# Row scaling of a softmax: from VectorE to GpSimd for all but the last three groups

## The chip, the cores and the metric

The kernel runs on one core of one Trainium2 chip. The time is device time in microseconds (us). Every ratio compares runs with a granted clock of 1.0. The *span* is the length of the profiled execution; the measured time is some 1.9 us longer. A *period* is the time from the start of one group of rows to the start of the next on the same engine.

## The reference

```python
x = randn(16, 1024, 512)                      # float32
x_max = np.max(x, axis=-1, keepdims=True)
exp_x = np.exp(x - x_max)
out = exp_x / np.sum(exp_x, axis=-1, keepdims=True)
```

It is 16384 independent softmax rows of 512 values: 33.55 MB in, 33.55 MB out.

## The kernel before

The kernel handles 128 softmax rows at a time, one per partition. Such a slab of 128 x 512 values is called a "row" from here on, and there are 128 of them. They come in ten chunks of 3, 5, 8 and then 16 rows, all into one big tile `held` that is worked on in place. Chunks are cut into groups of at most 8 rows, which makes 17 groups, numbered 0 to 16. Per group VectorE takes the negated maxima, ScalarE the exponentials with their sums, VectorE the reciprocals and then, row by row, the scaling. Loads are issued from SyncE. Stores are issued from ScalarE's own stream, so ScalarE's exponentials stand behind a store that waits.

```python
CHUNKS = [(3, 0), (5, 3), (8, 8), (16, 16), (16, 32), ...]   # rows, place in held
GROUP = 8
FINISH_BEFORE = (1, 2, 3)          # finish the small chunks before the next one starts
STORE_ROWS = {3: 8, 4: 8, 5: 8}    # these chunks are stored in halves, the later ones whole

    def rowmax(g):   # VectorE
        nc.vector.reduce_max(out=shift[g], in_=place[k][:, a:b, :], axis=AX, negate=True)

    def exps(g):     # ScalarE, one instruction per row
        for r in range(a, b):
            nc.scalar.activation(..., func=EXP, bias=shift[g][...], accum_out=sums[g][...])

    def scale(g):
        nc.vector.reciprocal(out=recip, in_=sums[g])
        for r in range(a, b):
            nc.vector.tensor_scalar_mul(out=place[k][:, r, :], in0=place[k][:, r, :],
                                        scalar1=recip[:, r - a : r - a + 1])
        if since is not None:
            nc.scalar.dma_start(out=dst[k][:, since:b, :], in_=place[k][:, since:b, :])
        # ... (the last two loads are issued behind two of the stores)

        for g in ...:              # the main loop
            # ... (for the small chunks, scale(waiting) comes first)
            rowmax(g); exps(g)
            if waiting is not None: scale(waiting)     # the group before
            waiting = g
        scale(waiting)
```

## Time and profile before

| | before |
|---|---|
| time, median of 6 fast runs | 161.48 us |
| span | 159.6 us |
| busy: VectorE (DVE), ScalarE (ACT), GpSimd (POOL) | 123.9, 93.3, 0.2 us |
| DMA | 67.13 MB, 421 GB/s on average over the span |
| last store issued | 144.93 us |

Engine names in the profile are DVE for VectorE, ACT for ScalarE, POOL for GpSimd. The prediction below shows the lines of this profile and how they are read.

### The profile page before, as it was taken

How to read it: one execution, taken by the hardware profiler on the slowest of the kernel's cores; microseconds unless marked ns; L12 is line 12 of the kernel's file. 1: busy time of each engine (PE TensorE's matmuls, PEld its weight loads, DVE VectorE, ACT ScalarE, POOL GpSimd, SP SyncE). 2: the span in 40 equal slices, each digit the busy share in tenths (PEclk: the TensorE clock that was granted, in tenths of full speed). 3: DMA queues.
4: the chain of work that ended last, by engine and by line, in shares of the span. 5: the costliest groups of instructions: out<-in, count | busy, mean ns of one | idle time of the engine just before them, and what ended most of it. 6: DMA issues, size and time to landing. Idle time of an engine off the chain costs nothing.

```text
span 159.6 us, 511 instructions
## 1 busy us (share of the span) xinstructions
DVE 123.9 (78%) x162; ACT 93.3 (58%) x257; POOL 0.2 (0%) x4
## 2 busy tenths in 40 slices
DVE  0482880799699999999999999999999999853000
ACT  0717119207994959595958687776868595940000
POOL 0000000000000000000000000000000000000000
DMA  7999999899999999999899999999999999999993
GB/s 267 443 456 432 399 414 466 375 404 467 411 446 411 485 419 396 439 411 493 378 448 439 411 497 411 405 444 402 435 444 485 411 402 468 435 402 419 485 411 164
DMA packets 3315, 67.13 MB, mean 421 GB/s; under 512 B 368, under 2 KB 368, under 8 KB 624
## 3 DMA queue, kind: packets, MB, share of 16 engines
q1 hardware_dynamic: 1440, 33.56, 49.4%
q10 hardware_dynamic: 1872, 33.56, 49.0%
q14 instruction: 3, 0.02, 0.0%
HBM read 33.55 MB, written 33.55 MB: 421 GB/s over the span
## 4 chain that ended last, share of the span: by engine, by line
DVE 71%; ACT 14%; issue 3%; DMA 3%; DVEq 0%; ACTq 0%
DVE shift L125 39%; DVE held L147 30%; ACT held L133 14%; DMA held<-in_x_dram 3%; DVE recip L145 2%; DVEq L199 0%; ACTq L133 0%
## 5 line engine op out<-in xcount | busy, mean ns | idle before, releaser
L133 ACT ACTIVATE held<-held,shift 128x512 f32<-128x512 f32 x128 | 90.5, 708 | 43.4 <-DVE shift L125 33.3
L125 DVE TENSOR_REDUCE shift<-held 128x8 f32<-128x4096 f32 (+2 forms) x17 | 70.7, 4164 | 4.6 <-DMA held<-in_x_dram 4.6
L147 DVE TENSOR_SCALAR held<-held,recip 128x512 f32<-128x512 f32 x128 | 52.2, 482 | 0.6
L133 ACT ACTIVATION_READ_ACCUMULATOR held<-held,shift 128x1 f32 x128 | 23.9, 187 | 0.0
L145 DVE RECIPROCAL recip<-sums 128x8 f32<-128x8 f32 (+2 forms) x17 | 3.3, 195 | 15.8 <-ACT held L133 15.8
L133 ACT ACT_TABLE_LOAD x1 | 1.3, 1283 | 4.7 <-DMA held<-in_x_dram 4.7
L188 POOL MEMSET const-bfloat16-1.0<- 128x1 bf16 x1 | 0.1, 103 | 0.0
L188 POOL MEMSET const-uint8-127<- 128x1 uint8 x1 | 0.1, 102 | 0.0
L188 POOL MEMSET const-float32-1.0<- 128x1 f32 x1 | 0.1, 100 | 0.0
L188 POOL MEMSET const-float32-0.0<- 128x1 f32 x1 | 0.1, 99 | 0.2 <-issue 0.2
## 6 DMA issues: line engine op xcount, KB each, us to landing
held<-in_x_dram SPq DMA_DIRECT2D x7, 4096.0 KB, 41.8
out_dram<-held ACTq DMA_DIRECT2D x4, 4096.0 KB, 20.9
out_dram<-held ACTq DMA_DIRECT2D x7, 2048.0 KB, 35.3
held<-in_x_dram SPq DMA_DIRECT2D x1, 2048.0 KB, 11.7
held<-in_x_dram SPq DMA_DIRECT2D x1, 1280.0 KB, 7.2
out_dram<-held ACTq DMA_DIRECT2D x1, 1280.0 KB, 19.9
held<-in_x_dram SPq DMA_DIRECT2D x1, 768.0 KB, 4.6
out_dram<-held ACTq DMA_DIRECT2D x1, 768.0 KB, 15.6
```

The costliest lines, as they stand in the source:

```text
L125: nc.vector.reduce_max(out=shift[g], in_=place[k][:, a:b, :], axis=AX, negate=True)
L133: nc.scalar.activation(out=place[k][:, r, :], in_=place[k][:, r, :], func=EXP, bias=shift[g][:, r - a : r - a + 1], scale=1.0, accum_out=s ...
L145: nc.vector.reciprocal(out=recip, in_=sums[g])
L147: nc.vector.tensor_scalar_mul(out=place[k][:, r, :], in0=place[k][:, r, :], scalar1=recip[:, r - a : r - a + 1],)
L188: nc = _bacc.Bacc("TRN2", target_bir_lowering=False, num_devices=1)
```

## The change

The intent is to relieve VectorE, which heads the chain of work, by an engine that does nothing: GpSimd multiplies a whole group by its reciprocals in one instruction, with the reciprocal of each row repeated along the row by a step of 0 in the access pattern. The last three groups stay on VectorE.

```diff
+ON_VECTOR = 3
 ...
         nc.vector.reciprocal(out=recip, in_=sums[g])
-        for r in range(a, b):
+        on_pool = g < len(groups) - ON_VECTOR
+        if on_pool:
+            nc.gpsimd.tensor_tensor(
+                out=place[k][:, a:b, :],
+                in0=place[k][:, a:b, :],
+                in1=recip.unsqueeze(2).to_broadcast([P, b - a, d]),
+                op=mybir.AluOpType.mult,
+            )
+        for r in () if on_pool else range(a, b):
             nc.vector.tensor_scalar_mul(
```

## The prediction

> **What bounds the kernel now.** I read the page first (engine shares, slices, queues), then the chain that ended last, the timeline of the last 20 us, and a table of stretches. From the page:
>
> ```profile
> span 159.6 us, 511 instructions
> DVE 123.9 (78%) x162; ACT 93.3 (58%) x257; POOL 0.2 (0%) x4
> DMA  7999999899999999999899999999999999999993
> q1 hardware_dynamic: 1440, 33.56, 49.4%
> q10 hardware_dynamic: 1872, 33.56, 49.0%
> L133 ACT ACTIVATE held<-held,shift 128x512 f32<-128x512 f32 x128 | 90.5, 708 | 43.4 <-DVE shift L125 33.3
> L125 DVE TENSOR_REDUCE shift<-held 128x8 f32<-128x4096 f32 (+2 forms) x17 | 70.7, 4164 | 4.6 <-DMA held<-in_x_dram 4.6
> L147 DVE TENSOR_SCALAR held<-held,recip 128x512 f32<-128x512 f32 x128 | 52.2, 482 | 0.6
> ```
>
> GpSimd is free and VectorE is the busiest engine, so moving 128 multiplications off it looks like an easy gain. But the load queue (q1) and the store queue (q10) together hold the 16 DMA engines for 49.4 + 49.0 = 98.4% of the span. The kernel must move 2 x 33.56 MB whatever computes it. VectorE's chain and the transfers are balanced: both are nearly full.
>
> The chain of work, in order of time, repeats one period for as long as there are rows:
>
> ```profile
> 23.20 0.02 issue
> 23.23 5.75 ACT held L133 x16
> ...
> 69.33 4.33 DVE shift L125
> 73.66 0.12 DVE recip L145
> 73.78 0.02 issue
> 73.81 3.26 DVE held L147 x8
> 77.07 4.33 DVE shift L125
> ```
>
> A group of 8 rows costs VectorE 4.33 (maximum) + 0.14 (reciprocal) + 3.26 (scaling) = 7.73 us; ScalarE needs 5.75 us for its exponentials. So VectorE sets the pace of the stores: 2.10 MB in 7.73 us is 271 GB/s, less than the DMA engines move, but loads use the rest. The stretches show it:
>
> ```profile
> 60.00:100.00 40.00, 39.82 (x55) 30.09 (x85) 0.00 (x0) 1.00 1.00 432
> 100.00:130.00 30.00, 29.86 (x39) 22.07 (x62) 0.00 (x0) 1.00 1.01 435
> 130.00:145.00 15.00, 12.36 (x23) 9.37 (x28) 0.00 (x0) 1.00 0.98 424
> 145.00:160.00 15.00, 0.00 (x0) 0.00 (x0) 0.00 (x0) 1.00 0.83 356
> ```
>
> (Columns after the stretch: its length; busy VectorE, ScalarE, GpSimd; clock; DMA share; GB/s.) In the last stretch 356 GB/s x 15 us = 5.34 MB still moves. The last store, of 4.19 MB, is issued at 144.93 by the timeline:
>
> ```profile
> 141.64 3.26 DVE L147 TENSOR_SCALAR held<-held,recip 128x512 f32<-128x512 f32 x8
> 144.93 0.34 ACTq L153 DMA_DIRECT2D out_dram<-held  x1
> ```
>
> So only 5.34 - 4.19 = 1.15 MB, or 2.7 us at 430 GB/s, is queued ahead of it. That is the whole slack: **a last store that is issued over 2 to 3 us later moves the end one for one.** With an empty queue I estimate the end at issue + 13.5 us: 9.8 us of transfer (4.19 MB at 430 GB/s), about 2.2 us from the last packet to the end of the span (the queue is quiet from about 157.4 to 159.6), and about 1.5 us to start.
>
> **What the Trainium skill says.** (1) "GPSIMD Engine Reference", section 3.1: tensor_tensor at N = 2048 fp32 takes 4497 ns on GpSimd, against 2293 on VectorE, about 2.6 cycles per element at 1.2 GHz, because both inputs share one read port. A broadcast second input is still a second input. The trace before has no GpSimd arithmetic (4 memsets), so it can't confirm this. (2) "SBUF — State Buffer", "Who interferes with whom": GpSimd's port pair is VectorE's second pair, an exclusive lock for a whole instruction; tensor_scalar in a 2-port mode takes it, tensor_reduce never does on trn2. The trace agrees that the scaling is in a two-element mode: 3.26 us for 8 x 512 elements is 0.80 ns each, the maximum 4.33 us for 4096, 1.06 ns each. (3) The same page, "A bandwidth-pool intuition that's wrong": 436 GB/s is the ceiling of DMA to SBUF; it also gives about 358 GB/s for HBM. The trace has 432 to 435, so it sits at the first and above the second.
>
> **The change, part by part.**
>
> *Removed from VectorE*: 14 of 17 scalings, 104 of 128 rows; 104 x 0.407 us (3.26/8) = 42.3 us. The maxima (70.7), reciprocals (3.3) and 24 rows of scaling (9.8) stay: 84 us. VectorE stops being the pace: 4.5 us per full group.
>
> *Added on GpSimd*: two groups of 1536 and 2560 elements and twelve of 4096. My estimate from (1): 4096 x 2.6 / 1.2 GHz = 8.87 us, plus 0.06 (4497 less 4437, the fixed part of the same row), plus a hop between engines: **D = 9.0 us per 8 rows**. That replaces 3.26 us of VectorE. GpSimd then needs 13 x 9.0 = 117 us for its 104 rows, more than any engine before in one period: 9.0 against 7.73.
>
> *Moved*: the instruction order shows that stores stay in ScalarE's stream and now wait for GpSimd; the exponentials behind them wait too. That matters at the start, where each small chunk is finished before the next one's exponentials.
>
> Walking through it: reciprocal of group 0 at 8.84 (as before); GpSimd 3 rows, 3.4, to 12.3; exponentials of the next 5 rows 3.64, to 16.0; reciprocal 16.2; GpSimd 5.6, to 21.9; exponentials 5.75, to 27.7; GpSimd from 27.9 to 36.9; exponentials to 42.7; fourth group on GpSimd 42.9 to 51.9. From there exponentials (5.75) hide under GpSimd (9.0), and ten more groups follow without a gap: the last GpSimd group ends at 51.9 + 90 = 141.9, the one before at 132.9.
>
> The tail: ScalarE's store of the eighth chunk waits until 132.9, then come the exponentials of group 14 (from 0) to 138.7 and its reciprocal at 138.9. Its VectorE scaling meets the last GpSimd group, which holds the lock until 141.9: it runs 141.9 to 145.2. The maximum of group 16 stands behind it: 149.5. Exponentials to 155.3, reciprocal and scaling to 158.8: **last store at 158.8**, 13.9 us later than before. If there is no lock, 3 us less: 155.8. The ninth chunk's store goes out at about 145.3 and is through by 157.1, so the last one finds an empty queue. End of the span: 158.8 + 13.5 = 172.3, or 169.3 without the lock. The measured time is 161.46 - 159.6 = 1.9 above the span: 174.2 or 171.2. I say **173.0 us**, 7.1% slower.
>
> **The rivals.**
>
> *A: GpSimd is quick enough and nothing happens.* If the multiplication ran near one element per cycle (D about 4.5), or anything up to about 7.7, GpSimd would keep VectorE's old pace, and the transfers would still set the end: 160 to 162 us. For it: the added instruction is one per 8 rows, so dispatch is paid once, and one input is a broadcast. Keeping just three groups on VectorE suggests that the author didn't think GpSimd starved. Against: the page lays the cost on two inputs, not on dispatch.
>
> *B: VectorE was the real limit and DMA merely keeps it company, so it gets faster.* The chain speaks for it (71% VectorE). Against: DMA is at 424 to 435 GB/s in every stretch from 10 to 145 us. At 436 throughout, 67.1 MB need 153.9 us, plus some 2 us at each end, plus 1.9: about 160 us, 1% at best. Over 2% (158.2) is nearly excluded.
>
> *C: GpSimd is dearer than the page's row*, by the lock, the in-place write, or the broadcast pattern. Each 0.1 us on D is carried by 12 full-group equivalents between the start and the last store but one (3 + 5 + 11 x 8 = 96 rows): 1.2 us at the end. D = 10 makes 185 us. A one-time cost before GpSimd's first multiplication (there is one extra setup instruction ahead of it) would add up to its own length, unless it runs in the idle 8.8 us at the start, as I expect.
>
> **Range and chances.** The end is 173.0 + 12 x (D - 9.0), until the floor of about 161. D between 8.4 and 9.7 gives 166 to 181; with 1.5 us each way for the lock I take 164 to 182. Slower by over 2% means over 164.7, D above about 8.3: I give 0.83. A floor result (rival A) has 0.15, faster 0.02.
>
> **What would show the steps right or wrong.** Right: GpSimd over 110 us busy, its 4096-element instructions starting 9.0 us apart from about 43 us on; stores following them; VectorE near 84 us busy; idle DMA slices from about 130 us on; the last store issued at 156 to 159; the first tensor_scalar of group 14 held until GpSimd's last instruction ends. The maxima should keep their 4.33 us beside GpSimd, since they take no second port. Wrong: a GpSimd spacing below 7.7 us with the DMA slices full to the end (A); a span under 157 us with DMA above 436 GB/s (B); a spacing of 10 or more, or a long first multiplication (C). If the spacing is 9.0 but the last store isn't late, my order of waits is wrong, most likely in which exponentials stand behind a store.

## The result

The changed kernel takes 161.47 us (median of 6), the kernel before 161.48. The ratio is 0.9998, with a 95% interval of 0.9985 to 1.0011. (A ratio here is the mean time of one kernel's fast runs over that of the other's of the same rounds, so not quite the ratio of the medians.) It is the same time to a tenth of a per cent; the prediction of 173 us was wrong.

The time is equal, but the inside is not. The page of the changed kernel:

```profile
span 159.6 us, 442 instructions
DVE 82.6 (52%) x58; ACT 92.9 (58%) x257; POOL 91.2 (57%) x18
DMA  7999999999999999999999999989999999999994
q1 hardware_dynamic: 1440, 33.56, 49.6%
q10 hardware_dynamic: 1872, 33.56, 49.0%
L150 POOL TENSOR_TENSOR held<-held,recip 128x4096 f32<-128x4096 f32 (+2 forms) x14 | 91.0, 6529 | 25.8 <-DVE recip L147 25.8
```

VectorE went from 123.9 to 82.6 us, as foreseen (84). GpSimd took on 91 us, not the 117 foreseen. The two DMA queues hold their engines for 98.6% of the span, against 98.4% before. The groups with their shapes kept apart give the size of GpSimd's instructions (busy us, mean ns of one):

```profile
L150 POOL TENSOR_TENSOR held<-held,recip 128x4096 f32<-128x4096 f32 x12 | 83.8, 7017 | 13.1 <-DVE recip L147 13.1
L150 POOL TENSOR_TENSOR held<-held,recip 128x2560 f32<-128x2560 f32 x1 | 4.5, 4455 | 4.4 <-DVE recip L147 4.4
L150 POOL TENSOR_TENSOR held<-held,recip 128x1536 f32<-128x1536 f32 x1 | 2.7, 2746 | 8.3 <-DVE recip L147 8.3
```

One fits a line through them: (7017 - 2746) / (4096 - 1536) = 1.668 ns per element and 0.184 us fixed. The timeline of GpSimd has eleven full groups in 76.76 us without a gap, 6.98 us each:

```profile
8.73 2.75 POOL L150 TENSOR_TENSOR held<-held,recip 128x1536 f32<-128x1536 f32 x1 [8.29 <-DVE recip L147]
...
40.46 76.76 POOL L150 TENSOR_TENSOR held<-held,recip 128x4096 f32<-128x4096 f32 x11 [6.54 <-DVE recip L147]
```

That is quicker than VectorE's old period of 7.73 us, so the stores go out earlier. The last four by ScalarE's timeline:

```profile
96.32 0.34 ACTq L163 DMA_DIRECT2D out_dram<-held  x1
110.27 0.34 ACTq L163 DMA_DIRECT2D out_dram<-held  x1
120.35 0.34 ACTq L163 DMA_DIRECT2D out_dram<-held  x1
134.00 0.34 ACTq L163 DMA_DIRECT2D out_dram<-held  x1
```

The last store is issued at 134.0 us instead of 144.9: the engines are 10.9 us ahead of before. The end doesn't move. The stretches say why (busy VectorE, ScalarE, GpSimd; clock; DMA share; GB/s):

```profile
100.00:130.00 30.00, 20.53 (x23) 24.85 (x71) 17.21 (x3) 1.00 1.02 439
130.00:145.00 15.00, 3.46 (x9) 0.38 (x2) 0.00 (x0) 1.00 0.98 424
145.00:160.00 15.00, 0.00 (x0) 0.00 (x0) 0.00 (x0) 1.00 0.83 356
```

The last two stretches have the same DMA share and the same GB/s as before, while the engines have little or nothing left to do (VectorE is busy for 3.46 us of the first 15, and then for none; before it was 12.36). What the engines gained became time that the stores spend in the queue: a 4 MB store takes a median of 29.1 us from issue to landing, against 20.9 before. The other end shows the same: the changed VectorE now waits for loads at two later maxima (0.21 and 0.81 us), which it never did before after the first chunk.

### The profile page after: what moved, and what is told of

Its sections match the earlier page's. It is cut to its first block, busy times and chain, and to the rows that moved or that the text cites. A ratio compares the mean times of both kernels' runs of the same rounds, so it can differ in the third digit from the quotient of the medians.

```text
span 159.6 us, 442 instructions
## 1 busy us (share of the span) xinstructions
DVE 82.6 (52%) x58; ACT 92.9 (58%) x257; POOL 91.2 (57%) x18
## 4 chain that ended last, share of the span: by engine, by line
POOL 51%; issue 12%; ACT 11%; DVE 7%; DMA 3%; ACTq 0%; DVEq 0%; POOLq 0%
POOL held L150 51%; ACT held L135 11%; DVE held L157 4%; DMA held<-in_x_dram 3%; DVE shift L127 3%; ACTq L163 0%; DVE recip L147 0%; DVEq L209 0%; POOLq L150 0%; DVEq L147 0%; ACTq L135 0%
## 5 line engine op out<-in xcount | busy, mean ns | idle before, releaser
L150 POOL TENSOR_TENSOR held<-held,recip 128x4096 f32<-128x4096 f32 (+2 forms) x14 | 91.0, 6529 | 25.8 <-DVE recip L147 25.8
L157 DVE TENSOR_SCALAR held<-held,recip 128x512 f32<-128x512 f32 x24 | 10.0, 491 | 0.1
## 6 DMA issues: line engine op xcount, KB each, us to landing
out_dram<-held ACTq DMA_DIRECT2D x4, 4096.0 KB, 29.1
```

The costliest lines, as they stand in the source:

```text
L150: nc.gpsimd.tensor_tensor(out=place[k][:, a:b, :], in0=place[k][:, a:b, :], in1=recip.unsqueeze(2).to_broadcast([P, b - a, d]), op=mybir.A ...
```

## The experiments

Theory T: the transfers set the end in both kernels, and the predicted loss failed to come because one number was too large, GpSimd's 9.0 us per group. Rivals: GpSimd's chain and VectorE's chain happen to cost the same (R); the walk through the waits (the prediction's schedule, from "Walking through it" to its tail) was wrong as well. A second question is why GpSimd was quicker than the skill's figure.

**No scaling at all.** The multiplications are removed on both engines; the result is wrong.

```diff
-        if on_pool:
-            nc.gpsimd.tensor_tensor(...)
-        for r in () if on_pool else range(a, b):
+        for r in ():
             nc.vector.tensor_scalar_mul(...)
```

> No engine scales at all (a wrong result on purpose: the exponentials are stored undivided); loads, maxima, exponentials, reciprocals and stores stay. Theory T (the transfers set the end in both kernels, so the work taken off VectorE and put on GpSimd had slack): within 0.3 us of both, 161.2 to 161.8 us, with the DMA slices full to the end and the last store issued far earlier than 134 us. Rival R (GpSimd's chain, 51% of the chain of the changed kernel, happens to cost just what VectorE's did): without it the time falls by several us, below 158.

Measured: 161.58 us, ratio 1.0007 (0.9995 to 1.0020). The last store goes out at 126.42 us, 18.5 us before that of the kernel before, and nothing is gained. Rival R falls: scaling that can be removed from both engines without effect sets nothing.

**Loads and stores alone.** Maxima, exponentials and reciprocals are removed too (wrong).

```diff
-            rowmax(g)
-            exps(g)
 ...
-        nc.vector.reciprocal(out=recip, in_=sums[g])
```

> Loads and stores alone, same sizes, same queues and order, no engine work (a wrong result on purpose). Theory T: 160 to 161.5 us, since 67.1 MB at the 430 to 435 GB/s seen in all stretches take 154 to 156 us and some 2 us at each end and 1.9 us outside the span come to it. Rival R: well below 158 us, as the engines would be what keeps the transfers from going faster.

Measured: 161.84 us, ratio 1.0020 (1.0007 to 1.0033), 0.3 us above the range that was expected. The page has no compute engine in it, and the same DMA row:

```profile
span 160.0 us, 65 instructions
POOL 0.2 (0%) x4
DMA  7999999899999999999999999999999999999993
HBM read 33.55 MB, written 33.55 MB: 420 GB/s over the span
```

A plain copy with these transfers takes as long as the softmax, so both kernels stand on the floor of their own transfers: the time below which engine work can't bring them. As long as these transfers stay as they are, no placement of engine work can be expected to gain anything.

**GpSimd at the size that was predicted.** A second multiplication into a scratch tile goes ahead of each GpSimd multiplication, so that a full group takes 9.0 us (1120 elements) or 8.0 us (528 elements). The result stays correct.

```diff
+PAD = 1120        # or 528
 ...
         if on_pool:
+            nc.gpsimd.tensor_tensor(
+                out=scratch[:, : PAD * (b - a) // 8],
+                in0=ones[:, : PAD * (b - a) // 8],
+                in1=recip[:, :1].to_broadcast([P, PAD * (b - a) // 8]),
+                op=mybir.AluOpType.mult,
+            )
             nc.gpsimd.tensor_tensor(...)
```

> Before each GpSimd multiplication, a second one of 1120 elements per 8 rows into a scratch tile, so that a full group takes GpSimd 9.0 us, the size that the prediction assumed, in place of the 6.97 measured. If only that size was wrong and the prediction's walk was right: about 173 us (171 to 176), the last store issued at 155.8 to 158.8 us, the VectorE scaling of group 14 held by GpSimd's last instruction, DMA idle before the end. If the walk was wrong too (stores not bound to GpSimd, or more slack than 3 us), below 168 us.

Measured: 174.36 us, ratio 1.0798 (1.0781 to 1.0814). The profile's period is 8.98 us (multiplications at 109.66 and 118.64). The tail of the VectorE timeline of this run:

```profile
140.90 0.20 DVE L151 RECIPROCAL recip<-sums 128x8 f32<-128x8 f32 x1 [7.81 <-ACT held L139]
141.14 5.55 DVE L167 TENSOR_SCALAR held<-held,recip 128x512 f32<-128x512 f32 x8
146.61 4.41 DVE L131 TENSOR_REDUCE shift<-held 128x8 f32<-128x4096 f32 x1
...
157.14 3.26 DVE L167 TENSOR_SCALAR held<-held,recip 128x512 f32<-128x512 f32 x8
```

and GpSimd's last instruction beside it:

```profile
136.61 7.02 POOL L160 TENSOR_TENSOR held<-held,recip 128x4096 f32<-128x4096 f32 x1
```

The scaling of group 14 starts at 141.14 while GpSimd works until 143.63, and its eight rows take 5.55 us; the next eight, with GpSimd done, take 3.26. One of the eight alone lasts 2.78 us against a median of 0.48. The last store is issued at 160.43, past the 155.8 to 158.8 that was expected, and the span ends 11.9 us later at 172.3; DMA moves only 280 GB/s from 130 to 160 us.

> The same with 528 elements: about 8.0 us per full group. The changed kernel issues its last store at 134.0 us with 6.97 us a group; twelve full-group equivalents at 1.03 us more put it at about 146.4 us, 1.5 us after the one of the kernel before (144.9), which had 1 to 3 us of slack. So: 161.4 to 163 us, the knee. Over 164 us if the lock or the order of waits adds to it; the prediction's own line (12 us per us on GpSimd from 173 at 9.0) gives 161.

Measured: 161.85 us, ratio 1.0021 (1.0007 to 1.0034). The period is 8.00 us, and the last store goes out at 147.70 us, 2.8 us later than in the kernel before, for 0.4 us more time. This is near the knee, the period from which a slower GpSimd shows in the time. From here to 8.98 us on GpSimd the time grows by 174.36 - 161.85 = 12.5 us.

**Two full inputs in place of a broadcast one.** Each full group is done as two multiplications of four rows by the other four (wrong).

```diff
+        if on_pool and b - a == 8:
+            lo, hi = place[k][:, a : a + 4, :], place[k][:, a + 4 : b, :]
+            nc.gpsimd.tensor_tensor(out=lo, in0=lo, in1=hi, op=mybir.AluOpType.mult)
+            nc.gpsimd.tensor_tensor(out=hi, in0=hi, in1=lo, op=mybir.AluOpType.mult)
```

> Each full group on GpSimd is done by two multiplications of 4 rows by the other 4 rows: 2048 elements, two different full inputs, no broadcast (a wrong result on purpose). Theory H2 (a two-input instruction costs GpSimd 2.0 cycles per element here, broadcast or not; the three sizes of the changed kernel fit 0.184 us + 1.668 ns per element): 0.184 + 2048 x 1.668 ns = 3.60 us each. Rival H1 (the broadcast input is what is cheap; two full inputs cost what the skill's page measured): about 4.5 us each.

> The same two instructions with add in place of mult, which is the operation that the skill's page measured at this very size (wrong on purpose). H2: 3.60 us, as for mult. Rival H3 (the add is slower than the multiplication): about 4.5 us.

Measured: 172.20 us with mult and 172.12 with add. The group of the first of the two multiplications:

```profile
L151 POOL TENSOR_TENSOR held<-held 128x2048 f32<-128x2048 f32 x12 | 54.2, 4516 | 12.6 <-ACT held L135 12.6
```

That is 4.516 us for 2048 elements, and 4.515 with add. My theory H2 (2.0 cycles whatever the input) and rival H3 (add is slower) both fall; H1 stands: two full inputs cost what the skill's page says.

**A repeated row in place of a repeated value.** The second input is one row of ones, repeated for the 8 rows: the outer step is 0, the inner one 1 (wrong on purpose; a single look).

```diff
-                in1=recip.unsqueeze(2).to_broadcast([P, b - a, d]),
+                in1=ones.unsqueeze(1).to_broadcast([P, b - a, d]),
```

> GpSimd's second input is one row of 512 ones repeated for each of the 8 rows, so that the innermost step is 1 and not 0 (wrong on purpose). H2: 7.0 us for 4096 elements, unchanged. H1, if the step of 0 is what is cheap: about 8.9 us.

Measured: 170.53 us.

```profile
L152 POOL TENSOR_TENSOR held<-held,ones 128x4096 f32<-128x4096 f32 x12 | 105.7, 8863 | 12.6 <-ACT held L137 12.6
```

A broadcast as such doesn't help: 8.86 us, against 7.02 with the inner step of 0. The elements, the instruction and the output tile are the same; the second input differs, with steps of 0 and 1 in place of 1 and 0 (and ones as its values). The inner step is what sorts all the runs: the padding multiplications, whose inner step is 0 too, lie on the line of the changed kernel (2055 ns for 1120 elements; the line gives 2052), and the patterns with an inner step of 1 are all dearer. Why GpSimd is quicker with a step of 0, no run shows. This run also stands for the change as I had priced it, about 8.80 us from start to start, and it is slow.

**One instruction per row.** Is the broadcasting over 8 rows what makes it cheap?

```diff
-        if on_pool:
+        for r in range(a, b) if on_pool else ():
             nc.gpsimd.tensor_tensor(
-                out=place[k][:, a:b, :],                                # in0 likewise
-                in1=recip.unsqueeze(2).to_broadcast([P, b - a, d]),
+                out=place[k][:, r, :],                                  # in0 likewise
+                in1=recip[:, r - a : r - a + 1].to_broadcast([P, d]),
```

> GpSimd does the same multiplication as 8 instructions of 512 elements with a broadcast of one value each, in place of one of 4096. From the fit: 0.184 + 512 x 1.668 ns = 1.04 us each, 8.3 us a group if nothing of it overlaps, about 8.0 if the start of one hides the end of the one before (the 4096-element ones start 0.05 us before the one ahead has ended). The last store then goes out at 134.0 + 12 x 1.0 to 1.35 us = 146 to 150 us; as 8.0 us a group gave 161.85 us, I expect 161.5 to 165 us. If each instruction costs much more than the fit, over 168.

Measured: 161.65 us, ratio 1.0011 (0.9995 to 1.0028). Sixteen take 16.02 us from first start to last end, so 8.0 us a group against 6.98 in one instruction: each of the seven further instructions costs 0.15 us. The last store goes out at 147.10, close to that of the padded run at 8.00 us (147.70).

**VectorE's own instruction on GpSimd**, one per row.

```diff
+        for r in range(a, b) if on_pool else ():
+            nc.gpsimd.tensor_scalar_mul(out=place[k][:, r, :], in0=place[k][:, r, :],
+                                        scalar1=recip[:, r - a : r - a + 1])
```

> GpSimd scales row by row with the instruction that VectorE uses (one tensor input, one value per partition). If one full input in place of two halves the cost per element (1.0 cycle, 0.83 ns): 0.43 + 0.18 = 0.61 us each, some 4.6 us a group; if the value per partition costs as much as a second tensor: 1.04 us, 8.0 us a group. The time is 161.4 to 161.8 us in the first case (transfers), up to 165 in the second.

Measured: 213.84 us, ratio 1.324 (1.322 to 1.326). Both guesses were too low:

```profile
L150 POOL TENSOR_SCALAR held<-held,recip 128x512 f32<-128x512 f32 x104 | 161.5, 1573 | 25.9 <-DVE recip L147 25.9
```

With one tensor input in place of two, a row takes 1.57 us in place of 1.07 (mean of the run before). Why is open: no run separates a fixed part from a part per element.

**GpSimd for all 17 groups.**

```diff
-ON_VECTOR = 3
+ON_VECTOR = 0
```

> GpSimd scales all 17 groups, the last three too. GpSimd's last multiplication ended at 117.2 us in the changed kernel; three more of 6.97 us end at 138.1 us at the earliest, with the last store then, some 4 us later than in the changed kernel and 7 us earlier than in the kernel before. As a last store at 147.7 us still gave 161.85 us: no change, 161.4 to 161.7 us. Rival (keeping the last groups on VectorE is what made the change come out even): over 163 us.

Measured: 161.52 us, ratio 1.0001 (0.9984 to 1.0017); the last store goes out at 138.19 us, as worked out. Keeping three groups on VectorE brings the last store forward by 4.2 us, which is worth nothing here.

**Both engines on the same group** (a single look): GpSimd scales rows 0 to 3, VectorE rows 4 to 7.

```diff
+        on_pool = on_pool and b - a == 8
+        m = a + 4 if on_pool else a
         # GpSimd: rows a to m
-        for r in () if on_pool else range(a, b):
+        for r in range(m, b):
```

> Each full group but the last three is split: GpSimd scales rows 0 to 3 (2048 elements, 3.60 us alone), VectorE rows 4 to 7 (8 x 0.41 / 2 = 1.63 us alone) at the same moment. If one locks the other out for whole instructions: either VectorE's four take about 5 us, first start to last end, or GpSimd's takes about 5.2. If they run side by side: 1.63 and 3.60. The time is that of the transfers, 161.4 to 162 us, either way.

Measured: 180.62 us. The timeline of one group:

```profile
73.06 0.19 DVE L147 RECIPROCAL recip<-sums 128x8 f32<-128x8 f32 x1
73.28 5.12 DVE L159 TENSOR_SCALAR held<-held,recip 128x512 f32<-128x512 f32 x4
73.32 3.60 POOL L152 TENSOR_TENSOR held<-held,recip 128x2048 f32<-128x2048 f32 x1 [5.99 <-DVE recip L147]
78.31 4.41 DVE L127 TENSOR_REDUCE shift<-held 128x8 f32<-128x4096 f32 x1
```

VectorE's four rows take 5.12 us, the sum of both (1.63 + 3.60 = 5.23) to a tenth; GpSimd's instruction keeps its 3.60. VectorE's longest scaling here lasts 3.93 us against a median of 0.48. So VectorE's first scaling is held until GpSimd's instruction is done. It is so in all twelve shared groups, although the trace has VectorE start 0.04 us before GpSimd each time; which of the two is held can't be read off these recorded starts. Nor is it always VectorE: in the run before last (VectorE's instruction on GpSimd) GpSimd's own rows take up to 2.11 us, median 1.56, where VectorE scales beside them. I expected no effect on the time and was wrong: VectorE's period grew to 9.58 us (reciprocals at 73.06 and 82.64), longer than before the change.

## Why the prediction was wrong

**The step that failed** is the first number of "Added on GpSimd": "D = 9.0 us per 8 rows". The prediction argued from the skill's row for two tensors that "a broadcast second input is still a second input". The runs show that it costs less than a full second input when its innermost step is 0: 2048 elements take 3.60 us with a step of 0 (the shared group) and 4.52 with two full inputs. Per element, from the sizes in each run, it is 1.67 ns against 8863 - 3428 = 5435 ns over 2560 elements, 2.12 ns, for the row of ones. A mis-sized term, then: 6.98 us in place of 9.0. Through twelve full-group equivalents it turned a kernel with slack into one that is late.

**What held.** The bound was read rightly: transfers and VectorE's chain balanced, and a floor near 161 us, which the copy confirms at 161.84. Rival A had it: it named "anything up to about 7.7" for D as harmless, and the truth lay at 6.98. The limit was even a little wider, as 8.00 us still gives 161.85. Rival B fell as argued, since even without compute the transfers are no faster. Of rival C, no one-time cost before the first multiplication is seen: it starts at 8.73 us, directly behind its reciprocal, and takes 2.75 us.

**The walk through the waits** was right, as the padded run shows: with 8.98 us a group it came to 174.36 us where the walk had 174.2 with the lock and 171.2 without. That the sum fits so well is partly luck. Two of its small terms were off and cancelled: the last store went out at 160.43 (walk: 158.8; the fourth group was already 1.9 us late, starting at 44.76 where the walk has 42.9), and from there to the end of the span it took 11.9 us (estimate: 13.5). The slope was taken as 12 us per us on D; from 8.00 to 8.98 the last store moved by 12.73 us, 13 per us, a little more, as the lock grows with D too: VectorE's held row took 1.79 us in the one run and 2.78 in the other.

**The lock** that the prediction took from the skill is there: 2.78 us for one row's scaling in the padded run and 3.93 in the shared one. In the changed kernel it cost only 0.26 us, because VectorE's first scaling (at 116.75) met the last 0.5 us of GpSimd's last instruction (to 117.22): 3.52 us for eight rows, not 3.26. Nor does the hold end with a single instruction: with one instruction per row on GpSimd, one scaling of VectorE lasted 1.72 us, through the rest of one GpSimd row and the whole of the next, its last. The maxima kept their time beside GpSimd (mean 4388 ns against 4414), as predicted.

**Where the 41 us went** that VectorE was spared: off the path at once. They brought the last store forward by 10.9 us, and the DMA queue, which had never run dry, swallowed that. The chances were badly placed: 0.83 on slower rested on one number that no trace had shown, with a threshold (8.3) that lay only 8% below it.

## What to carry to other kernels

First see what the transfers alone take: a copy with the same loads and stores gave 161.84 us here and settled in one experiment that no engine change could gain. Then ask of the engine that takes over work only whether its period stays within what the transfers hide (8.0 us here), and price it by the access pattern that is used, since a step of 0 made a 21% difference. Don't let VectorE scale and GpSimd multiply at the same moment: taking four of eight rows off VectorE that way made its period longer (9.58 us), while taking all eight made it shorter.

## What the Trainium skill lacked or had wrong

- "GPSIMD Engine Reference", section 3.1: its 4497 ns for tensor_tensor at N = 2048 is right for two full inputs (4516 ns here, the same for mult and add). Section 2.1 calls about 2.5 cycles per element the architectural floor for two inputs. With a second input whose innermost step is 0 the runs go below it: 3.60 us at 2048 and 7.02 us at 4096 elements, 1.668 ns per element, by estimate 2.0 cycles at the page's clock of 1.2 GHz. The page doesn't speak of an input with a step of 0. An outer step of 0 doesn't do it (8.86 us at 4096).
- The same page, section 4.1, has one-input instructions at roughly line rate. tensor_scalar with one value per partition took 1.57 us for 512 elements here, more than tensor_tensor with a broadcast value (1.07 us).
- "SBUF — State Buffer", section "A bandwidth-pool intuition that's wrong": its row of about 358 GB/s between HBM and a core, given there without a condition, did not bind: the copy alone moved 420 GB/s over its span, and the changed kernel 439 from 100 to 130 us. Other pages of the skill do say that a core which streams alone moves more, so this is a gap of the section and not of the skill.
